# Decoder trunk of two layers on one core: the short FFN group's second down pair as plain strips, the row factors' last steps, and the recurrence levels a chunk later

## The chip, the cores and the metric

The kernel runs on one core of a Trainium2 chip. The time is that of the whole program on the device, in microseconds; a run of it is one execution, and the number that counts is the median over runs. Beside the timed runs there is one profiled execution, whose own time is given with its span.

## The reference

Two decoder layers over 256 rows of width 2048, all in float32. Each layer mixes with a joint projection (sliding-window attention beside a gated linear recurrence), then has a SwiGLU feed-forward block and a gated input embedding; a norm over the row stands ahead of each block and behind the first two.

```python
def rms_norm(x, gain):
    y = xf * lax.rsqrt(jnp.mean(xf * xf, axis=-1, keepdims=True) + RMS_EPS)
    return (y * gain.astype(jnp.float32)).astype(x.dtype)
...
for i in range(DEPTH):
    h = rms_norm(x, pre_mix_gain[i])
    m = hybrid_mixer(h, positions, w_in[i], attn_sinks[i], lower_bounds[i],
                     attn_out_gain[i], hgrn_out_gain[i], w_out[i])
    x = x + rms_norm(m, post_mix_gain[i])
    h = rms_norm(x, pre_ffn_gain[i])
    f = (jax.nn.silu(h @ w_ffn_gate[i]) * (h @ w_ffn_up[i])) @ w_ffn_down[i]
    x = x + rms_norm(f, post_ffn_gain[i])
    gate = jax.nn.sigmoid(rms_norm(x, ple_gain[i]) @ w_ple_gate[i])
    x = x + (p[i] @ w_ple_proj[i]) * gate
```

The recurrence in the mixer works on chunks of rows with a decay between any two rows of a chunk and a state carried from chunk to chunk:

```python
b = jnp.cumsum(g_, axis=2)
decay = jnp.exp(jnp.where(causal[None, None, :, :, None], diff, MASK_VALUE))
a = jnp.einsum('bhtk,bhsk,bhtsk->bhts', q_, k_, decay)
o = jnp.einsum('bhts,bhsv->bhtv', a, v_) + \
    jnp.einsum('bhtk,bhkv->bhtv', q_ * jnp.exp(b), state)
```

## The kernel before

All large products are made on TensorE in a rounded float32 type (fp32r), with both operands split in two: a high part (the value rounded to fp32r) and a low part (what the rounding left). A product of blocks is then three matmuls: high by high, high by low, low by high. The activations stand as 128x128 blocks with the contraction on the partitions (the `ck` tiles, 256 columns for the two row tiles t = 0 and 1), and are split once. The weights stream in: one chunk is 256 rows by 512 columns, 512 KB, fetched by SP's queue into a `wr` buffer (10 of them), rounded by ScalarE into a `wh` buffer (L305, 7 of them), and its low part is made by VectorE into a `wl` buffer (L315, 7 of them). A chunk of a plain `strip` gives 12 matmuls of 128x512, six for t = 0 and six for t = 1; they add into two PSUM banks of the tag `acc`, of which there are four. Another four banks, tag `ms`, serve everything else.

`paired` does two strips side by side (two column blocks of 512, or the gate and the up weight) and saves one block product in eight for the first chunks. For chunks 0 and 1 it forms differences of the weight chunks (VectorE, L434, in place in the `wr` buffers), and multiplies seven blocks, not eight, by sums of activation blocks that were made beforehand (`mixed`, handed in as `sums`). Its seven weight operands each need a cast on ScalarE and a low part on VectorE. Partial results leave PSUM by four ScalarE copies (L427, `saved`) and meet in VectorE adds (L496 and the `done` function's adds). The chunks behind chunk 1 are done plainly, into banks that the program calls `acce`, `acca` (first strip) and `accc`, `accd` (second). With `half`, a fifth 128-row block pair goes the same way.

The FFN hidden width, 11 blocks of 512, is worked in groups `FF_GROUPS` of 2, 3, 3 and 3 blocks. For each group the gate and up products are made (`gated`), and then the down product of its blocks, in four column blocks s = 0 to 3 of 512, as two pairs; sums over the groups stand in `macc` (one SBUF tile for each s). The first group is the short one: two blocks, so 4 chunks of weights for each column block. Its `done` writes the sum of the PSUM bank and the saved part x into `macc` (L1252). The group's third hidden block, and the pair of `gated(2)` next, follow the short group's down product. In the last group s = 2 and 3 are already plain strips.

`sum_rstd` makes a row's factor (sum of squares to the power -1/2): the four partial sums `ss[:, 0:4]` are made one by one by ScalarE (`square_sum`, L199), and GpSimd adds them (L189, L190, L191), scales (L192) and takes the power (L194). `post_norm` uses it: VectorE adds the scaled block to the residual x (L557), TensorE transposes the result (L225), ScalarE and VectorE split it (L232, L234).

`Rec` is the recurrence, for two groups of four heads in each layer. It isn't a loop of its own: `levels` is a generator, and `tick`, which is called behind each weight chunk, moves it on by one `yield`. So its small matmuls lie between the chunks of the projections. Its stages are the diagonal blocks (L1065), two levels of four (`four`, L1024), the levels of 32 and 64 (L1095), the output of the first half (`out(0)`, L1126), the product across the halves (`px`, L1107, copied to `ax`) and the output of the second half. VectorE scales q and k between them (`up`, `prepare`, `up_four`).

The order of the instructions on each engine is set when the program is built, by a scheduler that goes by the order of the code, by its own estimates of when operands are ready, and by the edges that the code draws: `behind("pe")` puts an instruction behind the newest matmul of a weight chunk on its engine. On the chip each engine then works its list in that order, and waits on semaphores.

Of the kernel before, what the change touches and what calls it, by code (L numbers as in the profile page):

```python
# [24 lines left out]
W = 512  # L25
# [22 lines left out]
def decoder(ctx: ExitStack, tc: tile.TileContext, x, p, positions, w_in, attn_sinks,  # L48
# [137 lines left out]

    def sum_rstd(ss, n, name):
        v = tiny(1)
        G.tensor_tensor(v, ss[:, 0:1], ss[:, 1:2], op=ALU.add)  # L189
        G.tensor_tensor(v, v, ss[:, 2:3], op=ALU.add)  # L190
        G.tensor_tensor(v, v, ss[:, 3:4], op=ALU.add)  # L191
        G.tensor_scalar(v, v, 1.0 / n, EPS, op0=ALU.mult, op1=ALU.add)  # L192
        r = sm.tile([P, 1], F32, name=name)
        G.tensor_tensor(r, v, mhalf[:, 0:1], op=ALU.pow)  # L194
        return r
# [562 lines left out]
    for l in range(DEPTH):  # L758
# [164 lines left out]
        class Rec:  # L923
# [133 lines left out]

            def levels(s):
                yield
                pd = bank((P, NT, 4, 48))  # L1060
                for t in range(NT):
                    for h in range(4):
                        for j in range(4):
                            c = t * P + 32 * j
                            T.matmul(pd[32 * j:32 * j + 32, t, h], s.k[:, h, c:c + 32],  # L1065
                                     s.qd[:, h, t, j], start=True, stop=True)
                s.up(1)
                s.prepare(2)
                pv = pd.rearrange("p t h m -> p (t h) m")
# [31 lines left out]
                while 0 not in s.has_v:  # L1101
                    yield
                s.out(0)
                yield
                px = bank((P, 4, P))
                for h in range(4):
                    T.matmul(px[:, h], s.k[:, h, 0:P], s.q[:, h, P:2 * P], start=True, stop=True)  # L1107
# [123 lines left out]
        for gi, glen in enumerate(FF_GROUPS):  # L1231
# [11 lines left out]
            for s in range(4):  # L1243
                if gi == 0:
                    macc[s] = sp.tile([P, NT, W], F32, tag="ABCD"[s], name=f"macc{s}")
                if last:
                    gB = load_gain(post_ffn_gain[l], s * W)

                def done(t, ps, x, s=s, gB=gB if last else None):
                    m = macc[s][:, t]  # L1250
                    if gi == 0:
                        V.tensor_tensor(m, ps, x, op=ALU.add)  # L1252
                        return
                    V.tensor_tensor(m, ps, m, op=ALU.add)
                    if x is not None:
                        V.tensor_tensor(m, x, m, op=ALU.add)
                    if last:
                        square_sum(m, ssf[t][:, s:s + 1])
                        V.tensor_tensor(m, m, gB, op=ALU.mult)
                        if s == 3:  # L1260
                            post_norm(macc, ssf, t, nss, nxT, gain_cols(64, l, 16), (4, 3)[t])
                if last and s == 2:
                    fetch_x(sx[2])
                    pT2 = sp.tile([P, 2, 2, SEQ], F32R, tag="at", name="pT2")
                    pT = [pT2[:, 0], pT2[:, 1]]
                    for t in range(NT):
                        pn = nat()
                        nc.sync.dma_start(pn[:, 0:256], p[l, 0, t * P:(t + 1) * P, :])
                        split_T([pn[:, 0:P], pn[:, P:2 * P]], None, pT, t)
                dones.append(done)  # L1270
                if last and s >= 2:
                    strip(hid, w_ffn_down[l], s * W, lambda t, ps, done=done: done(t, ps, None),
                          nch=2 * glen, row0=ff0 * W, skew=4 if s == 3 else 0)
                elif s % 2:
                    paired(hid, lambda: hx[0], w_ffn_down[l], w_ffn_down[l], (s * W - W, s * W),
                           dones[s - 1], done, nch=2 * glen, row0=ff0 * W,
                           mixed_order=s == 1 and glen > 2)
# [80 lines left out]
```

## Time and profile before

| | |
|---|---|
| median of 3 runs | 2350.96 us |
| lowest, highest | 2347.1, 2351.49 us |
| the profiled execution's own time | 2349.07 us |
| its span | 2347.2 us |
| granted TensorE clock, mean over the span | 0.999 |
| TensorE busy (matmul) | 2326.7 us, 11719 records |
| VectorE busy | 1990.1 us |
| ScalarE busy | 1415.8 us |
| GpSimd busy | 120.5 us |

A row of the timeline has the start, the duration, the engine, the line of the code, the operation with what it writes and reads, and in brackets how long the engine was idle ahead of it and who released it. The records of matmuls overlap, since a matmul of 0.39 us starts before the one ahead of it has ended; what one costs is seen in the distance from one start to the next. A row with xN merges N instructions.

### The profile page before, as it was taken

Reading aid. Unit: us, or ns where it says so; the run is one execution under the profiler, and the core shown is the slowest. Engines: PE = TensorE matmul, PEld = TensorE weight load, DVE = VectorE, ACT = ScalarE, POOL = GpSimd, SP = SyncE. Lnnn points to the kernel's source line nnn. Section 1 sums busy time; section 2 is a strip of 40 time slices with the busy share of each in tenths; the row PEclk is TensorE's granted clock in tenths of the full one; section 3 lists DMA queues with packets and bytes.
Section 4 is the critical chain, followed back from the end, with each engine's and each line's share of the span. In section 5 each row is a group of like instructions: output and inputs, shape, how many; then the busy total and the mean of one; then the engine's idle time right before and its main releaser. Section 6 shows DMA issues by size and latency. Waiting matters only on the chain.

```text
span 2347.2 us, 33184 instructions
## 1 busy us (share of the span) xinstructions
PE 2326.7 (99%) x11719; PEld 1912.1 (81%) x11719; DVE 1990.1 (85%) x2559; ACT 1415.8 (60%) x2056; POOL 120.5 (5%) x229
## 2 busy tenths in 40 slices
PE   9999999999999999999999999999999999999999
PEld 7878887887888888888888788878778888888887
DVE  7786878898998999888877868788999989988885
ACT  6566656556656565656656666566566556565564
POOL 5100001000000000001010000010000000000010
PEclk9999999999999999999999999999999999999999
DMA  8666467576567665865776674666666575666743
GB/s 295 222 212 213 151 230 252 175 241 220 187 216 243 215 233 175 272 224 198 239 220 219 200 231 147 218 237 197 219 212 230 210 258 177 218 232 235 255 162 135
DMA packets 301671, 506.14 MB, mean 216 GB/s; under 512 B 23712, under 2 KB 69696, under 8 KB 301504
## 3 DMA queue, kind: packets, MB, share of 16 engines
q1 hardware_dynamic: 301200, 503.93, 64.4%
q8 instruction: 92, 1.51, 0.3%
q14 instruction: 75, 0.61, 0.1%
q0 software_dynamic: 64, 0.02, 0.0%
q10 hardware_dynamic: 240, 0.07, 0.0%
HBM read 474.57 MB, written 29.36 MB: 215 GB/s over the span
## 4 chain that ended last, share of the span: by engine, by line
PE 92%; DVE 5%; issue 1%; POOL 1%; ACT 1%; DMA 0%; SPq 0%; DVEq 0%; ACTq 0%; POOLq 0%
PE acc L330 9%; PE acc L331 9%; PE acc L333 9%; PE accc L422 5%; PE accc L421 5%; PE accc L418 5%; PE acca L422 4%; PE acce L422 4%; PE acca L421 4%; PE acca L418 4%; PE acce L418 4%; PE acce L421 4%; PE accd L422 3%; PE accd L418 3%; PE accd L421 3%; PE ms L418 3%
## 5 line engine op out<-in xcount | busy, mean ns | idle before, releaser
L305 ACT CAST wh<-wr 128x1024 fp32r<-128x1024 f32 x980 | 1007.5, 1052 | 701.8 <-DVE wr L434 204.4
L315 DVE TENSOR_TENSOR wl<-wr,wh 128x1024 fp32r<-128x1024 f32 x980 | 1164.0, 1220 | 225.7 <-ACT wh L305 216.8
L330 PE MATMUL acc<-wh,ck 128*128 128x512 f32 x1056 | 417.6, 396 | 0.3 <-ACT ck L203 0.3
L331 PE MATMUL acc<-wh,ck 128*128 128x512 f32 x1056 | 412.5, 391 | 0.4 <-DVE ck L204 0.4
L333 PE MATMUL acc<-wl,ck 128*128 128x512 f32 x1056 | 411.4, 391 | 0.8 <-DVE wl L315 0.8
L434 DVE TENSOR_TENSOR wr<-wr 128x1024 f32<-128x1024 f32 (+1 forms) x240 | 244.3, 1043 | 0.9
L333 PEld LDWEIGHTS acc<-wl,ck 128*128 128x128 f32 x1056 | 198.2, 188 | 43.3 <-DVE wl L315 1.7
L330 PEld LDWEIGHTS acc<-wh,ck 128*128 128x128 f32 x1056 | 198.3, 188 | 41.0 <-ACT ck L203 0.7
L331 PEld LDWEIGHTS acc<-wh,ck 128*128 128x128 f32 x1056 | 198.5, 188 | 40.2 <-DVE ck L204 0.9
L418 PE MATMUL acca<-wh,ck 128*128 128x512 f32 x468 | 182.9, 391 | 3.1 <-ACT wh L305 3.1
L422 PE MATMUL acca<-wl,ck 128*128 128x512 f32 x468 | 182.6, 390 | 1.0 <-DVE wl L315 1.0
L418 PE MATMUL acce<-wh,ck 128*128 128x512 f32 x468 | 182.9, 391 | 0.4 <-ACT wh L305 0.4
L422 PE MATMUL acce<-wl,ck 128*128 128x512 f32 x468 | 182.8, 391 | 0.3 <-DVE wl L315 0.3
L421 PE MATMUL acca<-wh,ck 128*128 128x512 f32 x468 | 182.5, 390 | 0.0
L421 PE MATMUL acce<-wh,ck 128*128 128x512 f32 x468 | 182.3, 390 | 0.0
L422 PE MATMUL accd<-wl,ck 128*128 128x512 f32 x368 | 144.7, 393 | 0.0
L418 PE MATMUL accd<-wh,ck 128*128 128x512 f32 x368 | 143.6, 390 | 0.0
L421 PE MATMUL accd<-wh,ck 128*128 128x512 f32 x368 | 143.2, 389 | 0.0
L421 PE MATMUL accc<-wh,ck 128*128 128x512 f32 x368 | 143.2, 389 | 0.0
L418 PE MATMUL accc<-wh,ck 128*128 128x512 f32 x368 | 143.2, 389 | 0.0
L422 PE MATMUL accc<-wl,ck 128*128 128x512 f32 x368 | 143.2, 389 | 0.0
L418 PEld LDWEIGHTS acca<-wh,ck 128*128 128x128 f32 x468 | 88.0, 188 | 23.0 <-ACT wh L305 4.8
(277 smaller groups left out, 3274.5 us busy)
## 6 DMA issues: line engine op xcount, KB each, us to landing
wr<-in_w_in_dram SPq DMA_DIRECT2D x176, 512.0 KB, 4.8
wr<-in_w_ffn_gate_dram SPq DMA_DIRECT2D x176, 512.0 KB, 5.8
wr<-in_w_ffn_up_dram SPq DMA_DIRECT2D x176, 512.0 KB, 5.9
wr<-in_w_ffn_down_dram SPq DMA_DIRECT2D x176, 512.0 KB, 7.3
wr<-in_w_out_dram SPq DMA_DIRECT2D x64, 512.0 KB, 4.8
wr<-in_w_ple_gate_dram SPq DMA_DIRECT2D x64, 512.0 KB, 5.2
turn<-nat SPq DMA_DIRECT2D x86, 256.0 KB, 2.4
nat<-turn SPq DMA_DIRECT2D x344, 64.0 KB, 3.6
```

The costliest lines, as they stand in the source:

```text
L305: marks["hi"] = S.copy(hi, raw)
L315: marks["lo"] = V.tensor_tensor(lo, raw, hi.bitcast(F32), op=ALU.subtract)
L330: T.matmul(ps[t], xh, hi[:, k], start=first, stop=False)
L331: T.matmul(ps[t], xl, hi[:, k], start=False, stop=False)
L333: marks[t, c] = marks["pe"] = T.matmul(ps[t], xh, lo[:, k], start=False, stop=last)
L418: T.matmul(ps, xh, hi[:, k], start=id(ps) not in opened, stop=False, skip_group_check=True)
L421: T.matmul(ps, xl, hi[:, k], start=False, stop=False, skip_group_check=True)
L422: marks["pe"] = T.matmul(ps, xh, lo[:, k], start=False, stop=k == ks[-1], skip_group_check=True)
L434: V.tensor_tensor(dst, p, q, op=ALU.subtract)
```

## The change

Three edits. First, in the short group (gi == 0) the columns s = 2 and 3 of the down product are two plain strips and no longer a pair; `done` is then called with no saved part, and ScalarE copies the bank to `macc`. Second, `sum_rstd` adds three of the partial sums, scales them, and brings in the fourth with one GpSimd instruction that multiplies it by 1/n and adds the rest as a per-partition scalar. Third, `levels` yields once more at its start, the diagonal matmuls are put behind the newest chunk's matmul, and the yield between `out(0)` and `px` is gone.

```diff
         v = tiny(1)
+        w = tiny(1)
         G.tensor_tensor(v, ss[:, 0:1], ss[:, 1:2], op=ALU.add)
         G.tensor_tensor(v, v, ss[:, 2:3], op=ALU.add)
-        G.tensor_tensor(v, v, ss[:, 3:4], op=ALU.add)
         G.tensor_scalar(v, v, 1.0 / n, EPS, op0=ALU.mult, op1=ALU.add)
+        G.tensor_scalar(w, ss[:, 3:4], 1.0 / n, v[:, 0:1], op0=ALU.mult, op1=ALU.add)
+        v = w
...
             def levels(s):
                 yield
+                yield
                 pd = bank((P, NT, 4, 48))
...
-                            T.matmul(pd[32 * j:32 * j + 32, t, h], s.k[:, h, c:c + 32],
-                                     s.qd[:, h, t, j], start=True, stop=True)
+                            with behind("pe"):
+                                T.matmul(pd[32 * j:32 * j + 32, t, h], s.k[:, h, c:c + 32],
+                                         s.qd[:, h, t, j], start=True, stop=True)
...
                 s.out(0)
-                yield
                 px = bank((P, 4, P))
...
                     if gi == 0:
-                        V.tensor_tensor(m, ps, x, op=ALU.add)
+                        if x is None:
+                            S.copy(m, ps)
+                        else:
+                            V.tensor_tensor(m, ps, x, op=ALU.add)
                         return
...
-                if last and s >= 2:
+                if (last or gi == 0) and s >= 2:
                     strip(hid, w_ffn_down[l], s * W, lambda t, ps, done=done: done(t, ps, None),
-                          nch=2 * glen, row0=ff0 * W, skew=4 if s == 3 else 0)
+                          nch=2 * glen, row0=ff0 * W, skew=4 if last and s == 3 else 0)
```

What this does to the lists of the engines is seen at three places. The lines of the changed code lie 2 to 6 further down (L434 becomes L436, L315 becomes L317, L1252 becomes L1256 and L1258, L1024 becomes L1026).

The first place is VectorE's list in layer 0 where the short group's first down pair ends and the second begins: the adds into `macc` are the first pair's end, the rows of `wr<-wr` the differences of the next pair's chunks, the rows of `wl` the low parts. Before:

```order
L1252 TENSOR_TENSOR macc_5148<-acce,nat 128x512
L434 TENSOR_TENSOR wr<-wr 128x1024 x2
L315 TENSOR_TENSOR wl<-wr,wh 128x1024 x2
L204 TENSOR_TENSOR ck<-nat,ck 128x4x128
L496 TENSOR_TENSOR nat<-ms,nat 128x512
L1252 TENSOR_TENSOR macc_5148<-acca,nat 128x512
L1252 TENSOR_TENSOR macc_5149<-accc,nat 128x512
L1252 TENSOR_TENSOR macc_5149<-accd,nat 128x512
L434 TENSOR_TENSOR wr<-wr 128x1024 x2
L315 TENSOR_TENSOR wl<-wr,wh 128x1024 x7
L1252 TENSOR_TENSOR macc_5326<-acce,nat 128x512
```

The same place in VectorE's list with the change:

```order
L1258 TENSOR_TENSOR macc_5156<-acce,nat 128x512
L317 TENSOR_TENSOR wl<-wr,wh 128x1024 x4
L206 TENSOR_TENSOR ck<-nat,ck 128x4x128
L498 TENSOR_TENSOR nat<-ms,nat 128x512
L1258 TENSOR_TENSOR macc_5156<-acca,nat 128x512
L1258 TENSOR_TENSOR macc_5157<-accc,nat 128x512
L1258 TENSOR_TENSOR macc_5157<-accd,nat 128x512
L317 TENSOR_TENSOR wl<-wr,wh 128x1024 x4
L436 TENSOR_TENSOR wr<-wr 128x1024
L317 TENSOR_TENSOR wl<-wr,wh 128x1024
L436 TENSOR_TENSOR wr<-wr 128x512 x2
L436 TENSOR_TENSOR wr<-wr 128x1024
```

The four differences of the second pair are gone, four low parts stand ahead of the first pair's last three adds where two differences and two low parts stood, and the differences that now follow belong to `gated(2)`.

The second place is TensorE's list in layer 0, first recurrence group, around the second level of four (the row with `qf`); the other rows are matmuls of one weight chunk, which has twelve, `acc0` for t = 0 and `acc1` for t = 1; buffer numbers are shown, and the first row is the chunk's second matmul. Before:

```order
L331 MATMUL acc0_1947<-wh_2015,ck_134 128x512
L333 MATMUL acc0_1947<-wl_2017,ck_133 128x512
L330 MATMUL acc0_1947<-wh_2015,ck_133 128x512
L1024 MATMUL ms_1967<-qf_1803,k_1033 32x48 x32
L331 MATMUL acc0_1947<-wh_2015,ck_134 128x512
```

With the change, on TensorE, from the sixth matmul of the same chunk on:

```order
L335 MATMUL acc0_1951<-wl_1975,ck_133 128x512
L332 MATMUL acc1_1952<-wh_1973,ck_133 128x512
L333 MATMUL acc1_1952<-wh_1973,ck_134 128x512
L335 MATMUL acc1_1952<-wl_1975,ck_133 128x512
L332 MATMUL acc1_1952<-wh_1973,ck_133 128x512
L333 MATMUL acc1_1952<-wh_1973,ck_134 128x512
L335 MATMUL acc1_1952<-wl_1975,ck_133 128x512
L1026 MATMUL ms_1989<-qf_1825,k_1035 32x48 x32
L332 MATMUL acc0_1951<-wh_2037,ck_135 128x512
```

The level of four stood behind the fourth matmul of the chunk and stands behind its twelfth now, eight matmuls later; in layer 1 the same stage moves by two. The diagonal blocks (L1065) keep their place in the first recurrence group of each layer and move by twelve matmuls in the second.

The third place is GpSimd's list at the post-norm of the mixer in layer 0, with buffer numbers (`ssm0` and `ssm1` are the partial sums of the two row tiles, `po0` and `po1` the factors). Before:

```order
L189 TENSOR_TENSOR tiny_3867<-ssm0_3201 128x1
L189 TENSOR_TENSOR tiny_3957<-ssm1_3202 128x1
L190 TENSOR_TENSOR tiny_3867<-tiny_3867,ssm0_3201 128x1
L190 TENSOR_TENSOR tiny_3957<-tiny_3957,ssm1_3202 128x1
L191 TENSOR_TENSOR tiny_3867<-tiny_3867,ssm0_3201 128x1
L192 TENSOR_SCALAR tiny_3867<-tiny_3867 128x1
L194 TENSOR_TENSOR po0_3872<-tiny_3867,mhalf_93 128x1
L191 TENSOR_TENSOR tiny_3957<-tiny_3957,ssm1_3202 128x1
L192 TENSOR_SCALAR tiny_3957<-tiny_3957 128x1
L194 TENSOR_TENSOR po1_3962<-tiny_3957,mhalf_93 128x1
```

With the change, on GpSimd:

```order
L190 TENSOR_TENSOR tiny_3871<-ssm0_3205 128x1
L191 TENSOR_TENSOR tiny_3871<-tiny_3871,ssm0_3205 128x1
L192 TENSOR_SCALAR tiny_3871<-tiny_3871 128x1
L193 TENSOR_SCALAR tiny_3872<-ssm0_3205,tiny_3871 128x1
L190 TENSOR_TENSOR tiny_3962<-ssm1_3206 128x1
L196 TENSOR_TENSOR po0_3877<-tiny_3872,mhalf_93 128x1
L191 TENSOR_TENSOR tiny_3962<-tiny_3962,ssm1_3206 128x1
L192 TENSOR_SCALAR tiny_3962<-tiny_3962 128x1
L193 TENSOR_SCALAR tiny_3963<-ssm1_3206,tiny_3962 128x1
L196 TENSOR_TENSOR po1_3968<-tiny_3963,mhalf_93 128x1
```

Behind the last partial sum of a row tile there stood an add, a scaling and the power; there stand the new two-operand scaling (L193) and the power now, and the second row tile's early steps have moved behind the first tile's last one. Over the whole program TensorE's list grows by 12 matmuls of 128x512, VectorE's shrinks by 24 instructions, ScalarE's by 6, GpSimd's and SP's keep their counts, and SP's transfers keep their order.

## The prediction

> **What bounds the kernel now.** I read the totals and the chain first, then TensorE's waits, then the timeline at the places where it waits.
>
> ```profile
> span 2347.2 us, 33184 instructions
> ...
> PE 2326.7 (99%) x11719; PEld 1912.1 (81%) x11719; DVE 1990.1 (85%) x2559; ACT 1415.8 (60%) x2056; POOL 120.5 (5%) x229
> ...
> PE 92%; DVE 5%; issue 1%; POOL 1%; ACT 1%; DMA 0%; SPq 0%; DVEq 0%; ACTq 0%; POOLq 0%
> ```
>
> TensorE is the bound: 99% busy and 92% of the chain. A change can take time only by giving it fewer matmuls or shorter waits, and any matmul added is paid in full. Its waits, longest first (total, times, longest):
>
> ```profile
> PE acca L418 <- ACT wh L305: 3.1, 4, 1.3
> PE ms L225 <- DVE x L557: 2.1, 4, 0.9
> ...
> PE ms L225 <- DVE ck L234: 1.4, 2, 0.7
> PE acca L422 <- DVE wl L315: 1.0, 2, 0.5
> ...
> PE ms L1065 <- DVE qd L979: 0.8, 2, 0.5
> ```
>
> The first and the fourth belong to products that `paired` makes, the second and third to the turning behind a post-norm, the last to the recurrence. Where are they, and what do they cost? This view counts the wait from a matmul's modelled end, so the cost is read from starts. Layer 0, the short group's second down pair (PE rows of the timeline):
>
> ```profile
> 530.11 0.39 PE L422 MATMUL acce<-wl,ck 128*128 128x512 f32 x1
> 531.79 0.50 PE L418 MATMUL acca<-wh,ck 128*128 128x512 f32 x1 [1.30 <-ACT wh L305]
> ...
> 533.82 0.63 PE L421 MATMUL acca<-wh,ck 128*128 128x512 f32 x1
> ...
> 537.20 0.39 PE L422 MATMUL acca<-wl,ck 128*128 128x512 f32 x1
> ...
> 539.92 0.39 PE L422 MATMUL acce<-wl,ck 128*128 128x512 f32 x1
> ```
>
> From 537.20 to 539.92 there are 12 matmuls: 2.72 us, 0.227 each. That is the price of a matmul. From 530.11 to 537.20 there are 15 starts, which should take 3.40 and take 7.09: 3.69 us are lost. Of that, 2.12 lie ahead of 533.82 (7 starts in 3.71), the wait for a cast. The rest, 1.57, lies in the 8 starts from 533.82 to 537.20, 0.42 apart: TensorE ran at half speed. Layer 1 has the same wait without the slow stretch; 5 starts, 3.22 less 1.13:
>
> ```profile
> 1696.67 0.39 PE L422 MATMUL acce<-wl,ck 128*128 128x512 f32 x1
> ...
> 1699.89 0.40 PE L422 MATMUL acca<-wl,ck 128*128 128x512 f32 x1
> ```
>
> so 2.09 lost. The stretches of both layers in the view of windows (the last but two columns are the granted clock):
>
> ```profile
> 527.00:540.00 13.00, 11.48 (x43) 8.69 (x42) 11.61 (x12) 9.18 (x11) 0.00 (x0) 0.87 0.58 206
> 1694.00:1707.00 13.00, 11.48 (x50) 8.84 (x49) 11.80 (x13) 10.91 (x13) 0.00 (x0) 1.00 0.47 162
> ```
>
> The clock is 0.87 in layer 0 and 1.00 in layer 1, at the same work. The head of the next pair, `gated(2)`, waits too:
>
> ```profile
> 556.25 0.39 PE L422 MATMUL acce<-wl,ck 128*128 128x512 f32 x1
> ...
> 562.81 0.40 PE L418 MATMUL acca<-wh,ck 128*128 128x512 f32 x1
> ...
> 1721.24 0.39 PE L422 MATMUL acce<-wl,ck 128*128 128x512 f32 x1
> ...
> 1727.82 0.39 PE L418 MATMUL acca<-wh,ck 128*128 128x512 f32 x1
> ```
>
> 21 starts in 6.56 and in 6.58 us, against 4.77: 1.8 lost in each layer. So around the short group's second pair TensorE loses 3.69 + 2.09 + 1.80 + 1.80 = 9.4 us.
>
> **The pair made plain: what it adds.** A pair multiplies 7 blocks where strips multiply 8; a block is 6 matmuls, so each layer gains 6 and the program 12, as the lists of the engines say: 2.72 us, all on the path.
>
> **What it takes away.** Who holds TensorE up there?
>
> ```profile
> 520.46 2.48 DVE L434 TENSOR_TENSOR wr<-wr 128x1024 f32<-128x1024 f32 x2
> ...
> 522.86 2.36 DVE L315 TENSOR_TENSOR wl<-wr,wh 128x1024 fp32r<-128x1024 f32 x2
> ...
> 526.34 0.68 DVE L1252 TENSOR_TENSOR macc<-acca,nat 128x512 f32<-128x512 f32 x1
> ...
> 528.13 2.48 DVE L434 TENSOR_TENSOR wr<-wr 128x1024 f32<-128x1024 f32 x2
> ...
> 530.70 7.68 ACT L305 CAST wh<-wr 128x1024 fp32r<-128x1024 f32 x8 [0.94 <-DVE wr L434]
> ```
>
> VectorE is behind. The differences at 528.13 end at 530.61, the cast starts at 530.70, and the matmul that needs it at 531.79. The plain strips need no difference: a chunk is cast and split as it lands. For each layer VectorE loses 4 differences of 1.24, 3 low parts of 1.18 (7 operands become 4), one add (L496) and four `macc` adds of 0.68: 12 instructions, 11.9 us; the count agrees with the 24 fewer in its list. ScalarE loses 3 casts and 4 copies and gets 4 copies, so 3 casts fewer, and the new copies stand in its list behind the casts that the strips need. I take both stalls of 2.1, the slow stretch behind one of them, and the two of 1.8 as gone: the head of `gated(2)` waits because VectorE comes late out of the pair, and with 11.9 us less work behind the same number of weight tiles it comes early.
>
> What is late next? The strips' banks. The first, for t = 0, is by the program's waits that of `acce`, free when the row at 520.46 starts. The one for t = 1 is that of `acca`, freed by the add at 526.34. Ahead of that add the list now has four low parts, 4 x 1.18 = 4.72, where two differences and two low parts stood, 2.48 + 2.36 = 4.84; so it still ends at about 527.0. The first pair's last matmul on TensorE is
>
> ```profile
> 526.48 0.39 PE L422 MATMUL accd<-wl,ck 128*128 128x512 f32 x1
> ```
>
> Two of the second pair's matmuls had been put ahead of it and are gone, so the strip begins at 526.71 - 0.45 = 526.26 and wants the second bank six matmuls later, at 527.6: 0.6 us of slack. I price this at nothing; a slip past that is a rival below. The transfers keep their order on SP, and buffers come free no later than before, since no chunk is kept for differences. Seven buffers of low parts hold more than a strip's four chunks, so its weights are ready.
>
> **The row factor's last step.** Behind the mixer, layer 0 (GpSimd, VectorE and TensorE rows):
>
> ```profile
> 380.00 1.22 DVE L315 TENSOR_TENSOR wl<-wr,wh 128x1024 fp32r<-128x1024 f32 x1
> ...
> 380.98 0.89 POOL L191 TENSOR_TENSOR tiny<-tiny,ssm 128x1 f32<-128x1 f32 x1 [12.95 <-ACT junk L199]
> ...
> 381.95 0.19 POOL L192 TENSOR_SCALAR tiny<-tiny 128x1 f32<-128x1 f32 x1
> ...
> 382.23 0.56 POOL L194 TENSOR_TENSOR po<-tiny,mhalf 128x1 f32<-128x1 f32 x1
> 382.36 0.39 PE L333 MATMUL acc<-wl,ck 128*128 128x512 f32 x1
> ...
> 382.82 2.74 DVE L557 SCALAR_TENSOR_TENSOR x<-mg,po,x 128x512 f32<-128x512 f32 x4 [1.00 <-POOL po L194]
> ...
> 383.63 1.32 PE L225 MATMUL ms<-ident,x 128*128 128x128 f32 x8 [0.88 <-DVE x L557]
> ```
>
> TensorE stands from 382.36 to 383.63, 1.27 where 0.23 is due, at the end of a chain: last partial sum, add, scaling, power, x. With the change the chain has two GpSimd steps, not three. A scaling with a per-partition scalar isn't in the trace. If it takes the add's long slot (380.98 to 381.95), what goes is the scaling's, 382.23 - 381.95 = 0.28; if the scaling's short one, the add's 0.97. The lower end is a form slower than both: 0.56, the power's length, in place of 0.19 on top of the long slot, gives 0.28 - 0.37, a loss of 0.1. I take 0.28, since the step that comes first after the long idle is the long one here. The waits list has four such waits for x: 4 x 0.28 = 1.1 us. Ends: 0.4 lost (4 x 0.1), and 2.1 gained, the whole of the waits for x.
>
> [...]
>
> **The levels a chunk later.** The diagonal blocks keep their place in the first recurrence group, so their waits (0.8 in the list) stay. The second level of four moves by eight matmuls in layer 0, 1.8 us, and by two in layer 1, 0.45:
>
> ```profile
> 166.27 0.39 PE L330 MATMUL acc<-wh,ck 128*128 128x512 f32 x1
> 166.68 0.89 PE L1024 MATMUL ms<-qf,k 128*32 128x48 f32 x64
> ...
> 1333.96 0.39 PE L330 MATMUL acc<-wh,ck 128*128 128x512 f32 x1
> 1334.58 0.89 PE L1024 MATMUL ms<-qf,k 128*32 128x48 f32 x64 [0.23 <-DVE qf L1012]
> ```
>
> It started 0.41 and 0.62 behind the matmul ahead of it, where 0.23 is due: 0.18 + 0.39 = 0.6 us, and both shifts cover it. In the second recurrence group nothing waits in the waits list, and a shift by twelve there gives nothing. The cross product `px` keeps its place and now follows `out(0)` at once; its scaling of k moves a chunk closer to it, 12 x 0.227 = 2.7 us, and it has two chunks today, so it stays covered. If that cover went, it would cost at most 2.7 in each of four groups. The gain could be 0.8 more, should the diagonal blocks' operand come earlier.
>
> **The sum**, against the profiled execution's own 2349.07 us: + 2.72 - 9.4 - 1.1 - 0.6 = - 8.4, so 2340.7 us. That execution lies 1.9 below the median of the runs shown, 2350.96, and 2.0 above the lowest. What lies outside its span, 1.9 us, I leave as it is. Against the median the forecast is 10.3 less, 0.44%. A difference of 0.2% (4.7 us) is about what a measurement of this kernel can tell from none.
>
> The clock's part in this: a stretch at half speed costs 1.6 us, and one layer of the two had it behind the same wait. [...]
>
> **Rivals.**
> 1. The stall only moves: the strips run well, but the head of `gated(2)` goes on waiting, because its own differences, casts and low parts are what bounds it and not the backlog. For it: both layers lose the same 1.8 there, with the clock whole in one. Against: VectorE comes to that pair's differences with 11.9 us less behind it. 2340.7 + 3.6 = 2344.3 us.
> 2. The banks: the strip's t = 1 bank is freed late. The add that frees it stands in one list behind four low parts and a split of the hidden block that waits for a transfer; a slip over 0.6 us is a wait in each layer. If it grows to what was there, 2.1 in each layer, with a slow stretch behind both, 2340.7 + 4.2 + 3.2 = 2348.1 us: no difference.
> 3. The slow end: GpSimd's new form is far dearer than any 128x1 scaling seen. There is a precedent for a slow tiny step:
>
> ```profile
> L194 POOL TENSOR_TENSOR rx<-tiny,mhalf 128x1 f32<-128x1 f32 x4 | 9.4, 2360 | 0.2
> ```
>
> The same power of 128x1 takes 0.56 for `po` and 2.36 for `rx`. The step is on TensorE's path at four places, so each microsecond above the long slot costs 4; slower than the median by 0.2%, at 2355.7, needs 15 more, or 3.7 us a step beyond what I take; at 4.2 it is 2357.5 us. Against: two operands of one column each.
> 4. A slow stretch of the clock stays somewhere in the typical run: 2340.7 + 1.6 = 2342.3. It changes the number and not the verdict.
>
> **How the numbers follow.** The forecast, 0.50; with a slow stretch (rival 4), 0.13; rival 1, 0.17; rival 2, 0.16; rival 3, 0.04. The bound of 0.2% under the median is 2346.3: the forecast and rivals 1 and 4 are under it, 0.80 for faster; rival 2 gives 0.16 for the same; rival 3 gives 0.04 for slower. Range: downward, the full gain of the row factor (1.0 more), the diagonal blocks' 0.8 and the 2.0 by which the lowest run shown lies under the profiled one give 2336.9, so 2336.5; upward, rival 1 with a slow stretch is 2345.9, so 2346.5. That leaves out rivals 2 and 3.
>
> **What would show it.** In the changed kernel's profile TensorE must have no wait for a cast or low part between the first pair's end and `gated(2)`, and the clock be 1.00 there; between the start of the short group's down product and some product of the third group the time must shrink by 5.49 - 1.36 = 4.1 us in layer 0 and 3.89 - 1.36 = 2.5 in layer 1. The wait ahead of the turning (L225) must be 0.28 shorter, at 1.0 from start to start, and the second level of four must start 0.23 behind its neighbour. The forecast is wrong if the first matmul into the second strip bank is late, if `gated(2)` still waits, or if VectorE's new room lets something else of the same queue start so early that it takes the casts' place.

## The result, and the profile after

The median of 11 runs is 2343.71 us (2341.8 to 2346.5), where the kernel before, run beside it, has 2350.96 (2347.1 to 2351.97): a ratio of 0.9973, with a 95% interval of 0.9964 to 0.9982. The forecast was 2340.7 us in 2336.5 to 2346.5, and faster. So the sign and the range hold, and the number is 3.0 us too low. The profiled execution's own time went from 2349.07 to 2343.71, 5.36 less, where the prediction's sum had 8.4.

The totals of the page after, and the first row of its chain:

```profile
span 2342.0 us, 33183 instructions
...
PE 2326.9 (99%) x11731; PEld 1914.5 (82%) x11731; DVE 1971.1 (84%) x2535; ACT 1412.5 (60%) x2050; POOL 114.7 (5%) x229
...
PE 91%; DVE 4%; DMA 2%; issue 1%; ACT 1%; POOL 1%; SPq 0%; DVEq 0%; ACTq 0%; POOLq 0%
```

TensorE has its 12 matmuls more, VectorE is 19 us less busy (the prediction's count, 11.9 in each layer, had 23.8), and TensorE is still the bound. Its list of waits after (total us, times, longest us):

```profile
PE ms L420 <- ACT nat L429: 2.0, 1, 2.0
PE ms L227 <- DVE x L559: 1.9, 4, 0.8
...
PE ms L227 <- DVE ck L236: 1.1, 2, 0.5
PE acc L335 <- DVE wl L317: 0.8, 2, 0.4
...
PE ms L1069 <- DVE qd L981: 0.3, 1, 0.3
```

The two waits for a cast and a low part at `acca`, 3.1 and 1.0 us before, are gone from it. What now leads it stood lower in the list before and is no part of the prediction's sum: a wait for a saved part (`nat`, L429).

The pair that follows the short group's down product is called `gated(2)` in the prediction and in some expectations. By the code it is `gated(3)`: the short group makes three hidden blocks ahead of its down product. The rows meant are the same, and the name does not enter the sum. TensorE's rows after in layer 0: the first pair's last matmul, the strip's first, its first into the second bank, and then two rows at the head of that next pair:

```profile
526.00 0.39 PE L424 MATMUL accd<-wl,ck 128*128 128x512 f32 x1
526.22 0.39 PE L332 MATMUL acc<-wh,ck 128*128 128x512 f32 x1
...
527.58 0.39 PE L332 MATMUL acc<-wh,ck 128*128 128x512 f32 x1
...
553.88 0.39 PE L424 MATMUL acce<-wl,ck 128*128 128x512 f32 x1
...
558.64 0.39 PE L424 MATMUL acca<-wl,ck 128*128 128x512 f32 x1
```

Every step of 0.22 or 0.23 is kept. At the head, 21 starts take 4.76 us, where they took 6.56. The view of windows over 13 us of the strips, layer 0 and layer 1 (the last but two columns are the clock):

```profile
526.00:539.00 13.00, 13.00 (x59) 10.78 (x58) 11.65 (x13) 6.36 (x8) 0.00 (x0) 1.00 0.93 343
1690.00:1703.00 13.00, 13.00 (x59) 10.78 (x58) 11.67 (x14) 6.50 (x8) 0.00 (x0) 1.00 0.96 352
```

TensorE is busy for the whole 13.00 us, where 11.48 stood, and the clock is 1.00 in both layers. VectorE is as busy as before there: a full list of VectorE's is not what held TensorE up, but the differences that stood in it ahead of a cast, as the run without them shows below.

The account by place, each read from starts against 0.227 us a matmul:

| place | forecast | measured |
|---|---|---|
| short group's second pair and what follows, layer 0 | -4.1 | -3.55 |
| the same, layer 1 | -2.5 | -2.03 |
| row factors | -1.1 | -1.4 |
| levels | -0.6 | -0.4 |
| last pair of the gated embedding, layer 0 | 0 | +2.14 |
| sum | -8.4 | -5.2 |

The two spans, 2347.2 and 2342.0, also differ by 5.2; the own times differ by 5.36, the rest lying outside the span. The last place in the table was not in the prediction. It is shown here by four views of the kernel after: SP's transfers, ScalarE, TensorE, and the window.

```profile
1111.80 0.46 SPq L301 DMA_DIRECT2D wr<-in_w_ple_proj_dram  x1
1124.54 4.98 SPq L301 DMA_DIRECT2D wr<-in_w_ple_gate_dram  x4
```

```profile
1130.28 1.05 ACT L307 CAST wh<-wr 128x1024 fp32r<-128x1024 f32 x1 [3.60 <-DMA wr<-in_w_ple_gate_dram]
...
1136.33 0.57 ACT L429 COPY nat<-ms 128x512 f32<-128x512 f32 x1
```

```profile
1134.52 0.39 PE L332 MATMUL ms<-wh,pT 128*128 128x512 f32 x1
1136.94 0.79 PE L420 MATMUL ms<-wh,sum 128*128 128x512 f32 x1 [2.04 <-ACT nat L429]
...
1140.43 0.39 PE L420 MATMUL acce<-wh,ck 128*128 128x512 f32 x1
```

```profile
1134.00:1141.00 7.00, 4.96 (x15) 3.66 (x15) 5.86 (x7) 5.51 (x9) 0.00 (x0) 0.76 0.85 274
```

SP issues no fetch from 1112.3 to 1124.54, since no `wr` buffer is free (the residual x holds four of the ten); before, it paused as long at this place, from 1116.6 to 1128.84. The chunks fetched then land late, ScalarE sits 3.60 us in front of the cast of one of them, and the copy that TensorE needs stands behind that cast in ScalarE's list. TensorE stands from 1134.52 to 1136.94. Then it runs at half speed (a granted clock of 0.50) to 1140.1. From 1134.52 to 1140.43 there are 9 starts: 5.91 us, with 2.04 due, 3.87 lost. Before, the same place lost less:

```profile
1138.83 0.39 PE L330 MATMUL ms<-wh,pT 128*128 128x512 f32 x1
1140.65 0.50 PE L418 MATMUL ms<-wh,sum 128*128 128x512 f32 x1 [1.44 <-ACT nat L427]
...
1142.60 0.39 PE L418 MATMUL acce<-wh,ck 128*128 128x512 f32 x1
```

9 starts in 3.77, so 1.73 lost, and no slow stretch. The two differ by 2.14.

Did the change make this wait longer? The traces don't show it. Four fetches are issued from 0.22 us behind the pair's first matmul on, in both kernels; what differs is how long they took to land. The two rows are from the DMA view of 16 us that end near the wait, after (1120 to 1136) and before (1124.3 to 1140.3); the last number is the median time to landing:

```profile
wr<-in_w_ple_gate_dram SPq DMA_DIRECT2D x5, 512.0 KB, 5.4
```

```profile
wr<-in_w_ple_gate_dram SPq DMA_DIRECT2D x5, 512.0 KB, 4.9
```

The levels alone, one of the runs below, have the old pair and the same fetches at this place, and yet a longer wait than either:

```profile
1136.93 0.39 PE L330 MATMUL ms<-wh,pT 128*128 128x512 f32 x1
1139.56 0.62 PE L418 MATMUL ms<-wh,sum 128*128 128x512 f32 x1 [2.24 <-ACT nat L427]
```

Its fourth fetch took 5.7 us to land where that of before took 4.9, and its gap from start to start is 2.63 us where that of before is 1.82: 0.8 each. Over the three profiled kernels with the old pair in full (before, row factors alone, levels alone) the gap is 1.82, 2.23 and 2.63; over four with the strips (the pair's edit alone, the changed kernel twice, the copies on VectorE) it is 2.38, 2.43, 2.01 and 2.11. So the 2.14 is a difference between two executions, which the change is not shown to have made; without it the account gives -7.4, where the medians differ by 7.2.

### The profile page after: what moved, and what is told of

Same layout as the page of the kernel before. It is cut to its first block, busy times and chain, and to the rows that moved or that the text cites. A ratio compares the mean times of both kernels' runs of the same rounds, so it can differ in the third digit from the quotient of the medians.

```text
span 2342.0 us, 33183 instructions
## 1 busy us (share of the span) xinstructions
PE 2326.9 (99%) x11731; PEld 1914.5 (82%) x11731; DVE 1971.1 (84%) x2535; ACT 1412.5 (60%) x2050; POOL 114.7 (5%) x229
## 4 chain that ended last, share of the span: by engine, by line
PE 91%; DVE 4%; DMA 2%; issue 1%; ACT 1%; POOL 1%; SPq 0%; DVEq 0%; ACTq 0%; POOLq 0%
PE acc L332 10%; PE acc L335 10%; PE acc L333 10%; PE accc L420 5%; PE accc L423 5%; PE accc L424 5%; PE acce L420 4%; PE acca L420 4%; PE acce L423 4%; PE acca L423 4%; PE acce L424 4%; PE acca L424 4%; PE accd L424 3%; PE accd L420 3%; PE accd L423 3%; PE ms L420 3%
## 5 line engine op out<-in xcount | busy, mean ns | idle before, releaser
L317 DVE TENSOR_TENSOR wl<-wr,wh 128x1024 fp32r<-128x1024 f32 x974 | 1160.1, 1222 | 242.3 <-ACT wh L307 230.5
L332 PE MATMUL acc<-wh,ck 128*128 128x512 f32 x1120 | 442.4, 395 | 0.7 <-ACT ck L205 0.7
L335 PE MATMUL acc<-wl,ck 128*128 128x512 f32 x1120 | 436.6, 391 | 0.8 <-DVE wl L317 0.8
L333 PE MATMUL acc<-wh,ck 128*128 128x512 f32 x1120 | 437.1, 391 | 0.1
L335 PEld LDWEIGHTS acc<-wl,ck 128*128 128x128 f32 x1120 | 210.2, 188 | 45.9 <-DVE wl L317 2.0
L332 PEld LDWEIGHTS acc<-wh,ck 128*128 128x128 f32 x1120 | 210.2, 188 | 44.0 <-ACT ck L205 0.9
L333 PEld LDWEIGHTS acc<-wh,ck 128*128 128x128 f32 x1120 | 210.4, 188 | 42.2 <-DVE ck L206 0.5
L436 DVE TENSOR_TENSOR wr<-wr 128x1024 f32<-128x1024 f32 (+1 forms) x232 | 235.5, 1039 | 1.2
L420 PE MATMUL acce<-wh,ck 128*128 128x512 f32 x456 | 177.9, 390 | 0.0
L420 PE MATMUL acca<-wh,ck 128*128 128x512 f32 x456 | 177.4, 389 | 0.0
L423 PE MATMUL acce<-wh,ck 128*128 128x512 f32 x456 | 177.4, 389 | 0.0
L423 PE MATMUL acca<-wh,ck 128*128 128x512 f32 x456 | 177.4, 389 | 0.0
L420 PE MATMUL accd<-wh,ck 128*128 128x512 f32 x360 | 140.5, 390 | 0.0
L423 PE MATMUL accd<-wh,ck 128*128 128x512 f32 x360 | 140.1, 389 | 0.0
L423 PE MATMUL accc<-wh,ck 128*128 128x512 f32 x360 | 140.1, 389 | 0.0
L420 PE MATMUL accc<-wh,ck 128*128 128x512 f32 x360 | 140.0, 389 | 0.0
L420 PEld LDWEIGHTS acce<-wh,ck 128*128 128x128 f32 x456 | 85.7, 188 | 18.0 <-ACT ck L205 0.3
```

The source lines that it names most:

```text
L317: marks["lo"] = V.tensor_tensor(lo, raw, hi.bitcast(F32), op=ALU.subtract)
L332: T.matmul(ps[t], xh, hi[:, k], start=first, stop=False)
L333: T.matmul(ps[t], xl, hi[:, k], start=False, stop=False)
L335: marks[t, c] = marks["pe"] = T.matmul(ps[t], xh, lo[:, k], start=False, stop=last)
L420: T.matmul(ps, xh, hi[:, k], start=id(ps) not in opened, stop=False, skip_group_check=True)
L423: T.matmul(ps, xl, hi[:, k], start=False, stop=False, skip_group_check=True)
```

## The experiments

Times are medians with the lowest and highest run, beside runs of the kernel before on the same chip (2350.33, 2351.24 and 2350.28 us in the three groups).

**Each part of the change alone.** First the short group's strips:

```diff
-                if last and s >= 2:
+                if (last or gi == 0) and s >= 2:
```

> Only the first edit: the short group's columns 2 and 3 as plain strips with ScalarE's copies; row factors and levels as before. Theory (the pair's work on VectorE held TensorE up): the losses of 2.1 and 1.8 us in each layer are gone as in the changed kernel, 12 matmuls of 0.227 are added, net -5.1 us against an execution of before with as many slow stretches of the clock, and on the median somewhat more (6 to 7), since the long waits that brought slow stretches are gone. Rival (the gain of the whole change came from the small edits, the pair gave its gain back in matmuls): within 1 us of before. The profile shows in the theory's case no wait for a cast or low part between the first pair and the second product behind it.

2345.49 us (2344.13 to 2347.9), ratio 0.9976 [0.9966, 0.9986]. That is 4.8 under the median of before, less than the 6 to 7 expected, though far from the rival's 1. In its trace the four waits of the pair and of the next pair's head are gone; the waits for x (2.1 us, 4 times) and of the diagonal blocks (0.8) stay as before. Then the row factors:

```diff
-        G.tensor_tensor(v, v, ss[:, 3:4], op=ALU.add)
         G.tensor_scalar(v, v, 1.0 / n, EPS, op0=ALU.mult, op1=ALU.add)
+        G.tensor_scalar(w, ss[:, 3:4], 1.0 / n, v[:, 0:1], op0=ALU.mult, op1=ALU.add)
```

> Only the second edit: the row factor finished in two GpSimd steps behind the last partial sum. Theory (the new step inherits the long slot of the add, and only the scaling's 0.28 us goes): each of the two post-norms of a layer gives 0.1 to 0.3 us, 0.9 us together, too little to be told from no change in the timed runs; in the profile the wait ahead of the turning behind the mixer is 1.15 from start to start where it was 1.27. Rival (the add's 0.97 goes): 2 us or more, that wait near 0.4.

2349.29 us (2347.68 to 2350.67), 0.9991 [0.9982, 0.9999]; behind the mixer TensorE has 1.13 from start to start, where 1.15 was expected. Then the levels:

```diff
             def levels(s):
                 yield
+                yield
...
                 s.out(0)
-                yield
```

> Only the third edit: the levels a chunk later, the cross product directly behind the first output. Theory: the second level of four no longer waits (0.18 and 0.39 us), the diagonal blocks wait 0.2 us less in each layer, 1.0 us together, not to be told from no change in the timed runs; nothing new waits. Rival (a cover goes): the cross product or the output of the second half waits up to 2.7 us in each of four recurrence groups, up to 11 us slower.

2349.3 us (2347.64 to 2352.54), 0.9997 [0.9988, 1.0006], which alone cannot be told from no change. The medians move by -4.8, -1.0 and -1.0, together -6.9, and the whole change by -7.2 against its own runs of before: as far as these intervals can tell, the parts add up, and the pair is most of it. The traces of the last two show who shortens the wait of the diagonal blocks. The row factors alone, then the levels alone:

```profile
PE ms L1067 <- DVE qd L981: 0.3, 1, 0.3
```

```profile
PE ms L1067 <- DVE qd L979: 0.8, 2, 0.5
```

It is the row factors: attention's norm uses `sum_rstd` too, and its factor comes earlier. The levels take only the second level of four's waits: from start to start its first matmul stood 0.41 and 0.62 us behind its neighbour, and stands 0.32 in both layers, 0.39 less in all. Where nothing waits this step takes 0.32 in the kernel before too (253.35 to 253.66).

**What held the cast.** The kernel before, with the differences of the short group's second pair left out, so that those columns' sums are not the reference's; casts, low parts, copies and matmuls all stay:

```diff
         def sub(dst, p, q):
+            if not diffs:
+                return
             V.tensor_tensor(dst, p, q, op=ALU.subtract)
...
-                            mixed_order=s == 1 and glen > 2)
+                            mixed_order=s == 1 and glen > 2, diffs=not (gi == 0 and s == 3))
```

> The kernel before with the four weight differences of the short group's second pair left out (so these columns' sums are not those of the reference); the seven products, their seven casts and low parts, the copies and adds stay. Theory (the differences are what holds the cast up, the cast started 0.09 us behind them): the 2.1 us lost ahead of acca are gone in both layers, and with 5 us less on VectorE for each layer most of the 1.8 at the head of the next pair goes too; no matmul is added, so -6 to -8 us against before. Rival (seven casts and low parts instead of four are the load, and ScalarE's copies stand in the way): TensorE still waits there for a cast, at least half of the 2.1 stays, and the gain is under 3 us.

2342.17 us (2341.63 to 2343.49), 0.9961 [0.9949, 0.9974]. TensorE's rows where the 2.1 us stood:

```profile
530.39 0.39 PE L422 MATMUL acce<-wl,ck 128*128 128x512 f32 x1
530.61 0.39 PE L418 MATMUL acca<-wh,ck 128*128 128x512 f32 x1
```

0.22 apart, where there were 1.68, and at the head of the next pair one wait is left in each layer, 0.16 and 0.15 us. So the four differences a layer, 5 us of VectorE, made nearly all of the four waits. No matmul was added or removed; this is the change's gain without its price.

**Who copies.** The changed kernel, with the copies into the sums on VectorE:

```diff
-                            S.copy(m, ps)
+                            V.tensor_copy(m, ps)
```

> The changed kernel, with the copies of the short group's plain strips into the sums made by VectorE and not by ScalarE; TensorE's and the transfers' lists stay as they are. Theory (what counts is that the differences and three low parts are gone from VectorE; 11.9 us of room in each layer is far more than four copies): no difference, a median within 1.7 us of the changed kernel's 2343.7, the lowest run near its 2341.8, and no wait of TensorE between the first pair's end and the head of gated(2). Rival (ScalarE's share matters: on VectorE the copies stand in one list with the low parts of the next pair): the head of gated(2) waits again, 0.5 to 1.8 us in each layer, 2344.7 to 2347.3.

2344.17 us (2341.68 to 2347.95), 0.9970 [0.9960, 0.9981], and no wait at the strips or the next pair's head. ScalarE's part in the change is worth nothing that can be measured; VectorE has room once the differences are gone.

**The place that was overlooked.** The changed kernel, with layer 0's last two column blocks of the gated embedding as strips, and without the sums of activations that the pair needed:

```diff
-        for s in (0, 1):
+        for s in (0, 1) if end else range(4):
...
-            strip(xT, w_ple_gate[l], s * W, gate_of(s, pa), skew=SKEW if s == 0 else 0)
+            strip(xT, w_ple_gate[l], s * W, gate_of(s, pa), skew=SKEW if s in (0, 3) else 0)
...
-        paired(xT, lambda: px, w_ple_gate[l], w_ple_gate[l], (2 * W, 3 * W),
+        if end: paired(xT, lambda: px, w_ple_gate[l], w_ple_gate[l], (2 * W, 3 * W),
```

> The changed kernel, with layer 0's last two column blocks of the gated embedding as two plain strips too, and no pair: 6 matmuls of 128x512 more, 1.36 us. Theory (what the forecast missed is this pair: TensorE waits 2.2 + 0.4 us in it for a saved part, and a stretch of slow clock, 1.57 us, follows in most executions): the wait and the stretch go, the typical run is 2.57 + 1.57 - 1.36 = 2.8 us lower, about 2341.0, and the lowest 2341.8 - 2.57 + 1.36 = 2340.6, with no row of the clock under 1.00 near 1137 us. First rival (the weights' transfers are what is late there, the saved part only stands behind a cast that waits for them): the wait turns up at another matmul of the strips, 2343.7 + 1.4 = 2345.1. Second rival (the slow stretch has nothing to do with that wait): the stretch turns up elsewhere, 2343.7 - 1.2 = 2342.5, with the runs as widely spread as before.

2341.23 us (2341.12 to 2343.02), 0.9960 [0.9947, 0.9972]; four of its five runs lie within 0.11 us. The same window:

```profile
1134.00:1141.00 7.00, 7.00 (x33) 5.79 (x32) 4.05 (x7) 3.18 (x5) 0.00 (x0) 1.00 1.00 306
```

TensorE has no gap and the clock is whole. This kernel and the changed one then ran once more, on one chip:

> The kernel with layer 0's last pair of the gated embedding plain, once more, beside the changed kernel. By the theory of the wait and the stretch: a median of about 2341.2, most runs within 0.3 of it, 2 to 2.5 below the changed kernel's median; by chance alone: no nearer to 2341.2 than to 2343.7.

> The changed kernel once more, on the same chip as the run with the embedding's pair plain. If its 2.5 us over that kernel are the wait and the slow stretch, its times again lie in steps of about 1.6 us from 2341.8 up, with a median of about 2343.7; if they were the chip's, both come out alike.

2341.64 us (2341.01 to 2343.42) for the embedding's pair plain, 2344.66 (2341.36 to 2346.54) for the changed kernel. The plain one is 3.0 lower, and it is the fastest version here that gives the reference's result. Most of its runs were expected within 0.3 of 2341.2; two of five were, and three within 0.5. The changed kernel's runs were expected in steps of about 1.6 with a median of 2343.7; they don't lie in such steps (four are between 2344.4 and 2344.9). The profiled execution of the changed kernel's repeat shows where else a slow stretch lies; the window of the first weights, in that repeat and then in the first profile of the changed kernel:

```profile
5.00:20.00 15.00, 13.75 (x59) 10.68 (x58) 10.62 (x14) 9.71 (x18) 11.76 (x57) 0.89 0.99 345
```

```profile
5.00:20.00 15.00, 14.12 (x69) 11.09 (x68) 11.70 (x15) 10.56 (x18) 13.20 (x57) 1.00 1.01 338
```

In the repeat the stretch lies at the start, and none follows the embedding's wait (1.8 us there, and a clock of 1.00 from 1134 to 1141). So a slow stretch followed that wait in one execution and lay at the start in another, and no version here changes the start.

**What a GpSimd step costs.** Two more dependent steps ahead of the power, in the post-norms' factors alone:

```diff
-        v = w
+        v = w; [G.tensor_scalar(v, v, 1.0, None, op0=ALU.mult) for _ in range(2 if name[:2] == "po" else 0)]
```

> The changed kernel, with two more GpSimd steps of 128x1 (a multiplication by 1.0, each dependent on the one before) ahead of the power in the factors of the two post-norms of each layer, 16 instructions. Theory (the chain on GpSimd ends last at all four places, and a step counts in full, 0.28 us from start to start): 0.56 more wait ahead of the turning at each place, 2.2 us in all, about 2345.9; the wait behind the FFN's last product, whose place in TensorE's list stays, goes from 0.69 to 1.25. Rival (only part of a step counts, as the 0.13 and 0.18 that the step taken away gave, since something else ends about as late): 0.25 to 0.36 a place, 1.0 to 1.4 in all, and 0.95 to 1.05 behind the FFN's product.

2348.68 us (2346.61 to 2349.91), 0.9988 [0.9979, 0.9997]: 5.0 over the changed kernel's median and 4.8 over its lowest, more than either theory had. Behind the FFN's last product, TensorE's wait rises by 0.60 and 0.62, so a step counts in full, 0.30. But at the FFN's first row tile, left out of both theories, it rises by 0.91 in each layer. GpSimd's rows there:

```profile
1067.63 1.12 POOL L193 TENSOR_SCALAR tiny<-ssf,tiny 128x1 f32<-128x1 f32 x1 [9.50 <-ACT junk L201]
1068.71 0.19 POOL L190 TENSOR_TENSOR tiny<-ssf 128x1 f32<-128x1 f32 x1
1068.86 0.22 POOL L194 TENSOR_SCALAR tiny<-tiny 128x1 f32<-128x1 f32 x1
1069.04 0.18 POOL L191 TENSOR_TENSOR tiny<-tiny,ssf 128x1 f32<-128x1 f32 x1
...
1069.75 0.57 POOL L196 TENSOR_TENSOR po<-tiny,mhalf 128x1 f32<-128x1 f32 x1
```

The other row tile's early steps (L190, L191) are put between this one's late ones, and the power starts 2.12 us behind L193, where it was 1.23. At the mixer's post-norm the turning also moved in TensorE's list, and 0.9 was lost in each layer. The chain is on the path at six places, not four: at the mixer's post-norm, at the FFN's first row tile and behind the FFN's last product, in each of two layers.

**Is plain better everywhere?** The embedding's version, with the short group's first pair plain as well, and the sums of activations made for that group left out:

```diff
-                if (last or gi == 0) and s >= 2:
+                if gi == 0 or last and s >= 2:
```

> The kernel with layer 0's last pair of the gated embedding plain, and now also the short group's first down pair as two plain strips in each layer, so that the group has no pair, and the sums of activations made for it are left out: 12 matmuls more, 2.72 us. Theory (a pair pays with VectorE's time and TensorE's waits, and gains 1.36 us of matmuls; plain is better only where the waits are longer than that): the first pair's waits are 0.19 + 0.25 us in each layer, 0.9 in all, so the time is 1.8 higher, 2341.2 + 1.8 = 2343.0. Rival (VectorE is what holds the whole stretch up, and each us taken from it there shows): the time stays at 2341.2 or falls.

2342.35 us (2341.92 to 2344.15), 0.9968 [0.9957, 0.9979]: 0.9 over its base's lowest (2341.01) and 1.1 over the median of its ten runs (2341.23); 1.3 to 1.4 between the profiled spans, none of which has a slow stretch behind its start. By the timed runs alone the two can't be told apart (0.9968 and 0.9967 beside the same runs of before), so this rests on the spans. The first pair's waits are gone, but 2.72 of matmuls costs more. The sign is the theory's; 0.5 of its 1.8 is missing in the spans, in waits too small to place.

## Why the prediction was right, and where it was off

- **The pair.** The four waits went, the slow stretch at 533 with them, the strips' banks came in time, and the price was 12 matmuls. Both layers together gave 5.58 and not 6.6. That one slow stretch was booked was chance: of the three profiled kernels with this pair in full, the one before has it in layer 0, the row factors alone have it in layer 1, and the levels alone in neither. The step that failed is the one that put the first pair's end at "526.71 - 0.45" and booked that shift at nothing. The two matmuls of the second pair that stood ahead of it were not idle company. They filled two waits for a low part; before, then after:

```profile
516.94 0.39 PE L418 MATMUL ms<-wh,ck 128*128 128x512 f32 x1
517.16 0.46 PE L422 MATMUL accd<-wl,ck 128*128 128x512 f32 x1
...
518.62 0.39 PE L421 MATMUL ms<-wh,ck 128*128 128x512 f32 x1
518.87 0.50 PE L422 MATMUL accd<-wl,ck 128*128 128x512 f32 x1
```

```profile
516.09 0.39 PE L423 MATMUL accd<-wh,ck 128*128 128x512 f32 x1
516.51 0.50 PE L424 MATMUL accd<-wl,ck 128*128 128x512 f32 x1
...
517.77 0.40 PE L423 MATMUL accd<-wh,ck 128*128 128x512 f32 x1
518.25 0.50 PE L424 MATMUL accd<-wl,ck 128*128 128x512 f32 x1
```

  VectorE delivers those low parts at the same moment of the pair as before, and TensorE now waits 0.19 + 0.25 us for them, in each layer: 0.9 of the 1.0 that is missing.
- **The banks' slack** was put at 0.6 us. The add that frees the second bank ended at 527.1, and the bank was wanted at 527.58: 0.5. Rivals 1 and 2 did not occur.
- **The row factors.** The price of the new step was chosen right, the long slot: in place of 0.89 and a scaling there is one step of 0.88. GpSimd and TensorE at the mixer's post-norm, after:

```profile
380.66 0.88 POOL L193 TENSOR_SCALAR tiny<-ssm,tiny 128x1 f32<-128x1 f32 x1 [12.20 <-ACT junk L201]
381.62 0.56 POOL L196 TENSOR_TENSOR po<-tiny,mhalf 128x1 f32<-128x1 f32 x1
381.88 0.39 PE L333 MATMUL acc<-wh,ck 128*128 128x512 f32 x1
383.02 0.66 PE L227 MATMUL ms<-ident,x 128*128 128x128 f32 x4 [0.76 <-DVE x L559]
```

  The power starts 0.96 behind the step, where 1.25 stood: 0.29 less, where 0.28 was forecast. From start to start TensorE has 1.14, not the 1.0 that was named, so only 0.13 of it shows there; the stretch of strips around it, 48.03 us before and 47.66 after, is 0.37 shorter, and the rest lies in the turning itself, which now has a matmul between its two halves. Behind the FFN it is 0.18 a layer, in the wait that the list gives as `ck`, L236. At the FFN's first row tile, which makes two of the four waits for x, nothing was gained: the new step takes 1.12 there and the other tile's first step slips in ahead of the power. What the list of places lacked was attention's norm: 0.42 over both layers. So that the sum came out at 1.4 beside a forecast of 1.1 is partly luck: two of the four places gave nothing, and places that were not among them gave 0.36 and 0.42.

  The choice was right, but the reason that the prediction gives beside it, that the step first after a long idle time is the long one, does not hold. In the trace before, every one of the 38 long steps ends 0.04 to 0.09 us behind the end of a VectorE instruction with two operands in SBUF (the last section has the count). The first of these rows, after, is a step of the same line that follows 10.13 us of idle time; VectorE was at rest from 366.42 to 367.65, and the step is short, 0.27 us. The second is VectorE's instruction that ran beside the step at 380.66, which ended 0.1 us behind it:

```profile
366.68 0.27 POOL L193 TENSOR_SCALAR tiny<-ssm,tiny 128x1 f32<-128x1 f32 x1 [10.13 <-ACT junk L201]
...
380.71 0.69 DVE L1187 TENSOR_TENSOR mg<-nat,gB 128x512 f32<-128x512 f32 x1
```

- **The levels**: 0.4 of 0.6. The prediction took 0.23 as due ahead of the level's first matmul, and 0.32 is due there, so its waits were 0.09 and 0.30 and not 0.18 and 0.39; the sign that it named, a start 0.23 behind the neighbour, came out as 0.32 with no wait. The 0.8 held open for the diagonal blocks was not theirs to give, as the levels alone show.
- **The place overlooked.** By the account this is most of the 3.0 us, though the change is not shown to have made it. The number rested on no slow stretch being left, and rival 4, with 0.13, had one "somewhere". The wait that it followed, 1.4 us, was in the waits list of before, and was passed over since the change does not touch it. By starts it cost 1.6 us before, 2.2 after, and with the same lists 1.8 in the repeat. It goes with the landing of its weights: in seven of the nine profiled executions with this pair the matmul that waits starts 2.3 us behind the landing of the fourth of the four fetches. Why they take longer in one execution than in another is left open. That it and the stretch cost what the account says is borne out by taking that pair away, with its differences and casts: 2.5 to 3.0 us off the median, though 1.36 us of matmuls were added. The range held since it left 5.8 upward, for rival 1 with a slow stretch; what took 3.0 of that was another wait, so that part is luck.

## What to carry to other kernels

A trick that saves matmuls pays with another engine's time, and is worth its one eighth only where that engine does not make TensorE wait for longer than the matmuls saved. Read it pair by pair: plain won where the waits were longer than 1.36 us, and lost where they were 0.4. Before booking work that vanishes as neutral, look whether it filled a wait. Before booking a wait that an execution shows, look whether another execution of the same lists has it. And read the waits that a change leaves alone too, since one that a slow stretch of the clock followed cost more than its own length (at the embedding's pair 3.87 us, of which 2.19 were the wait).

## What the runs showed of the hardware

A wait of TensorE's cost a second time in some executions: a slow stretch of the clock followed it. In the traces of before and of the changed kernel the clock's records show one such stretch behind a wait in each, of 3.41 us at half speed, worth about 1.6 us at full load (in the kernel before, 8 starts in 3.38 us, where 1.81 is due). Whether and how many of them an execution has is part of what sets it apart from the next: of the nine profiled executions with the embedding's pair, five have one behind its wait (the clock is 0.76 from 1134 to 1141 in the changed kernel) and four have not (1.00 over the same stretch in its repeat and with the copies on VectorE). Each run here has one profiled execution, so how much of the spread of times they make is not shown. The length of a wait did not decide it here: a gap of 2.42 us between starts was followed by a stretch (changed kernel, 1134.52), one of 2.99 us at the same place was not (the differences left out). What decides it is not shown.

Some small GpSimd steps lasted until the VectorE instruction that they ran beside had ended. In the trace before there are 96 additions and scalings of one column (L189 to L192). Of these 58 took 0.19 to 0.39 us. The other 38 took 0.48 to 2.11, and every one of them ended 0.04 to 0.09 us behind the end of a VectorE instruction with two operands in SBUF. One of them, with the two low parts that it ran beside:

```profile
144.21 2.35 DVE L315 TENSOR_TENSOR wl<-wr,wh 128x1024 fp32r<-128x1024 f32 x2
...
145.03 1.57 POOL L191 TENSOR_TENSOR tiny<-tiny,ssa 128x1 f32<-128x1 f32 x1 [2.85 <-ACT junk L199]
```

In the run with two more steps, a dependent step inside a chain took 0.30 from start to start.
